# A column mean over 8192 rows: the last group of rows in five pieces instead of four, in three banks instead of two

## The chip, the cores and the metric

The kernel runs on one core of a Trainium2 chip. The metric is the device time of one execution in microseconds (us). Before the change the median of 3 runs is 628.02 us (628.0 to 628.23).

## The reference

```python
def setup_inputs():
    return {"x": np.random.randn(8192, 8192).astype(np.float32)}

def reference(x):
    return np.mean(x, axis=0)
```

The input is 256 MB of float32 (MB and KB count 1024 here, where rates and totals of the profile count 1000), and every byte of it has to be read once. The output is one row of 8192 values.

## The kernel before

The 8192 rows are 64 groups of 128 rows, one row of a group on each of the 128 partitions. A group is 8192 columns wide, 4 MB, and a column range of 512 (F) is called a block, so that a group has 16 blocks. Groups 0 to 59 are loaded in pairs, 8 MB in one DMA, and groups 60 to 63 singly (`strips`, L62 to L68, says which rows of the input stand in which group; for the sum it does not matter).

**Buffers.** `bufs` has six slots of one group. Four (0 to 3) take turns as landing places, two slots for a pair. The other two are `both` (slot 4) and `acc` (slot 5). Pair 0 is loaded straight into `both` and `acc`. An extra tile `early` takes blocks 0 to 5 of group 60, which are loaded at the start: two blocks ahead of pair 0 and four behind the first pairs (`load_early`).

**Loads.** All loads are issued by SyncE in program order on one DMA queue (`load`, L51). Those into slots that are reused wait for the VectorE add that read the slots last. Every second load from the ninth on waits also for two loads eight and seven places ahead, so that semaphores can be used again.

**Adds.** VectorE does the sums over groups (`add`, L78). Pairs 2, 4 and 6 are added to the two slots `both` and `acc` at once, each by one wide add of up to 16384 columns; the third leaves out blocks 0 and 1, which TensorE sums. Then `both` is added to `acc`. From group 8 on each pair takes two adds: `both` = slot u + slot u+1, then `acc` = `acc` + `both`. A load's add waits through a no-op on ScalarE or GpSimd (L83), which waits for the load and for the add before it. GpSimd adds `early` to `acc` in two parts, after groups 24 and 32.

**The sum over partitions.** TensorE multiplies a block by a 128 x 32 matrix of 1/8192 (`product`, L98). The result stands in one of four column groups of the array (q = 0 to 3, `tile_position`), 32 partitions of a PSUM bank; four blocks with different q share a bank of 512 columns. Each product shows as two weight loads and two matmuls in the profile. Banks 0, 1 and 2 hold blocks 0 to 11. Blocks 12 to 15 are cut differently: their 2048 columns are seen as four quarters (j) of 512 columns, each with four strips (q) of W = 128 columns, and a product takes the strips q of some quarters (`chunks`, L159). So a bank gets the first three quarters (bank 3, 384 columns) and another the last quarter (bank 4, 128 columns).

**The end.** VectorE adds only a part of groups 60 to 62 to `acc`; the other blocks, and all of group 63, go through TensorE directly. Group 63 is loaded in four pieces of 8, 4, 3 and 1 blocks. The list `sums` is the order in which TensorE works: blocks 0 to 5 of `acc` and of group 61, blocks 0 to 9 of group 62, blocks 6 and 7 of `acc`, blocks 0 to 7 of group 63, blocks 8 to 11 of `acc` and then of group 63, and the chunks of `acc` and of group 63. All engines keep program order. ScalarE then copies banks 0, 1 and 2 to `res` and bank 3 to `fin`, VectorE copies bank 4 to `fin`. ScalarE stores bank 0, SyncE stores banks 1 and 2 and, last, `fin`. Ahead of each store SyncE runs no-ops that wait for what the store needs (`landed`, L45), because one instruction can take few waits.

Of the kernel before, what the change touches and what calls it, by code (L numbers as in the profile page):

```python
# [9 lines left out]
def kernel(  # L10
# [9 lines left out]
    F = 512  # L20
    W = F // 4
# [19 lines left out]
    banks = [psp.tile([P, F], f32, name=f"bank{b}") for b in range(5)]  # L41
# [56 lines left out]
    def product(b, q, cols, start, stop):  # L98
        dst = banks[b][32 * q:32 * q + 32, :]
        if b > 2:  # L100
            dst = dst.rearrange("p (j w) -> p j w", w=W)[:, :cols.shape[1], :]
        return tc.keep_in_program_order(nc.tensor.matmul(  # L102
            out=dst,
            lhsT=ones[:],
            rhs=cols,
            start=start,
            stop=stop,
            tile_position=(0, 32 * q),
            skip_group_check=True,
        )).ins  # L110
# [6 lines left out]
    for g in range(2, G - 4, 2):  # L117
        u = (g + 2) % 4
        dma = load_rows(g, u, 2)
        if g < 8:  # L120
            cols = slice(0 if g < 6 else 2 * F, N)
            add(sums2[:, :, cols], sums2[:, :, cols], bufs[:, u:u + 2, cols], [dma] + first)
            first = []
            if g == 4:
                load_early(2, E)
            if g == 6:
                for q in range(2):
                    for j in range(2):
                        product(0, q, bufs[:, u + j, q * F:(q + 1) * F], j == 0, False)
                add(acc, acc, both, [])  # L130
            continue
        add(both, bufs[:, u, :], bufs[:, u + 1, :], [dma])
        add(acc, acc, both, ahead)
        ahead = []
        if g in (24, 32):
            cols = slice(0, 2 * F) if g == 24 else slice(2 * F, E * F)
            ins = tc.keep_in_program_order(nc.gpsimd.tensor_add(  # L137
                out=acc[:, cols], in0=acc[:, cols], in1=early[:, cols])).ins
            tc.add_to_no_dep_group("early", ins)
            ahead = [joined] = [ins]  # L140
# [3 lines left out]
    for row, g, lo in [(r60, G - 4, E * F), (r61, G - 3, 0)]:  # L144
        add(acc[:, cols], acc[:, cols], row[:, cols], [load(row[:, lo:], rows(g)[:, lo:])])

    dma = load(r62, rows(G - 2))
    cols = slice(10 * F, N)
    add(acc[:, cols], acc[:, cols], r62[:, cols], [dma])
    for lo, hi in [(0, 8), (8, 12), (12, 15), (15, 16)]:  # L150
        load(r63[:, lo * F:hi * F], rows(G - 1)[:, lo * F:hi * F])
# [3 lines left out]
    def blocks(row, lo, hi):  # L155
        for i in range(lo, hi):
            sums.append((i // 4, i % 4, row[:, i * F:(i + 1) * F]))

    def chunks(row, lo, hi):  # L159
        for q in range(4):  # L160
            cols = row[:, 12 * F:].rearrange("p (j q w) -> p q j w", j=4, q=4)[:, q, lo:hi, :]
            sums.append((3 + lo // 3, q, cols))
# [12 lines left out]
    for n, (b, q, cols) in enumerate(sums):  # L175
        summed = product(b, q, cols, all(k[:2] != (b, q) for k in [(0, 0), (0, 1)] + sums[:n]),
# [14 lines left out]
    copied = copy(fin[:, :3 * W], banks[3][:, :3 * W])  # L191
    ended = nc.vector.tensor_copy(out=fin[:, 3 * W:], in_=banks[4][:, :W]).ins  # L192
    landed(*joins.values())
    landed(loads[-6])
    landed(*loads[-5:-3])
# [6 lines left out]
    landed(*loads[-3:-1])  # L202
    landed(loads[-1], s0)
    landed(s1, summed)
# [33 lines left out]
```

## Time and profile before

| | |
|---|---|
| runs (median of 3) | 628.02 us |
| the profiled execution: its span from first to last instruction (the only time that the profile gives for it) | 626.3 us |
| load queue, share of 16 DMA engines | 99.2% |
| HBM read | 268.44 MB (of 1000), 429 GB/s over the span |
| VectorE busy | 527.7 us |
| TensorE matmuls busy | 18.3 us |
| ScalarE, GpSimd busy | 3.7 us, 7.4 us |
| add of 16384 columns, mean of two | 17.2 us |
| add of 14336 columns (the third wide add) | 15.1 us |
| add of 8192 columns, mean of 53 | 8.7 us |
| last pieces of group 63: 2048, 1024, 768, 256 KB, issue to landing | 21.3, 23.2, 24.7, 24.8 us |

How to read it: busy times of the engines overlap, so they don't add up to the span. The chain of waits follows the work that ended last back to the start; 70% of it are DMAs, 28% adds of VectorE, 1% matmuls. "Issue to landing" of a load includes the time that it stands in the queue behind earlier loads. PE is TensorE's matmul, PEld its weight load, DVE VectorE, ACT ScalarE, POOL GpSimd, SPq SyncE's queue.

### The profile page before, as it was taken

The page shows a single profiled execution, that of the slowest core. Times are in us where ns is not written, and L with a number is a line of the kernel's source. Part 1 is how long each engine was busy: PE and PEld are TensorE (multiplying, and loading weights), DVE is VectorE, ACT ScalarE, POOL GpSimd, SP SyncE. Part 2 cuts the span into 40 slices and gives each one's busy share as a digit, 9 for nine tenths or more (in the row PEclk, how much of TensorE's full clock was granted, in tenths as well). Part 3 has the DMA queues.
Part 4 walks back from the last instruction along what each step waited for, and adds up shares of the span by engine and source line. Part 5 has one row for each costly group of instructions (what it writes and reads, how often), then busy time and mean ns, then how long its engine had stood idle before and what let it go on. Part 6 is the DMA issues. An engine that isn't in the chain of part 4 may idle for free.

```text
span 626.3 us, 464 instructions
## 1 busy us (share of the span) xinstructions
PE 18.3 (3%) x120; PEld 4.6 (1%) x120; DVE 527.7 (84%) x60; ACT 3.7 (1%) x6; POOL 7.4 (1%) x8
## 2 busy tenths in 40 slices
PE   0000020000000000000000000000000000000035
PEld 0000000000000000000000000000000000000001
DVE  0028979999988998888988899988898888998895
ACT  0000000000000000000000000000000000000001
POOL 0000000000000000010000200000000000000000
PEclk9999999999999999999999999999999999999999
DMA  9999999999999999999999999999999999999997
GB/s 393 444 402 434 437 469 402 469 402 465 406 448 423 440 431 423 448 410 460 406 465 402 469 402 469 402 469 402 469 402 465 406 448 423 423 448 406 431 435 305
DMA packets 5658, 268.50 MB, mean 429 GB/s; under 512 B 636, under 2 KB 652, under 8 KB 1048
## 3 DMA queue, kind: packets, MB, share of 16 engines
q1 hardware_dynamic: 5648, 268.46, 99.2%
q8 instruction: 1, 0.02, 0.0%
q10 hardware_dynamic: 8, 0.01, 0.0%
q14 instruction: 1, 0.01, 0.0%
HBM read 268.44 MB, written 0.03 MB: 429 GB/s over the span
## 4 chain that ended last, share of the span: by engine, by line
DMA 70%; DVE 28%; PE 1%; SPq 0%; issue 0%; ACTq 0%; POOLq 0%
DMA bufs<-in_x_dram 70%; DVE bufs L80 28%; PE bank L102 1%; SPq L52 0%; ACTq L83 0%; DVE fin L192 0%; POOLq L83 0%
## 5 line engine op out<-in xcount | busy, mean ns | idle before, releaser
L80 DVE TENSOR_TENSOR bufs<-bufs 128x8192 f32<-128x8192 f32 (+4 forms) x59 | 527.4, 8939 | 92.2 <-POOLq L83 52.3
L102 PE MATMUL bank<-bufs,ones 128*32 128x512 f32 (+2 forms) x120 | 18.3, 634 | 605.0 <-DVE bufs L80 517.7
L137 POOL TENSOR_TENSOR bufs<-bufs,early 128x1024 f32<-128x1024 f32 (+1 forms) x2 | 6.8, 3416 | 350.0 <-DVE bufs L80 350.0
L102 PEld LDWEIGHTS bank<-bufs,ones 128*32 128x32 f32 x120 | 4.6, 120 | 618.5 <-issue 610.7
L182 ACT COPY bufs<-bank 128x512 f32<-128x512 f32 x3 | 1.8, 586 | 618.2 <-PE bank L102 618.2
L192 DVE COPY fin<-bank 128x128 f32<-128x128 f32 x1 | 0.3, 292 | 3.8 <-PE bank L102 3.8
L115 ACT ACT_TABLE_LOAD x1 | 1.3, 1283 | 0.7 <-PEq L222 0.7
L182 ACT COPY fin<-bank 128x384 f32<-128x384 f32 x1 | 0.5, 480 | 1.0 <-PE bank L102 1.0
L115 ACT COPY warm<-ones 128x32 f32<-128x32 f32 x1 | 0.2, 217 | 0.0
L40 POOL TENSOR_TENSOR ready<-ones 128x1 f32<-128x1 f32 x1 | 0.2, 192 | 0.1
L37 POOL MEMSET ones<- 128x32 f32 x1 | 0.1, 124 | 0.3 <-POOLq L222 0.3
L222 POOL MEMSET const-bfloat16-1.0<- 128x1 bf16 x1 | 0.1, 101 | 0.0
L222 POOL MEMSET const-uint8-127<- 128x1 uint8 x1 | 0.1, 101 | 0.0
L222 POOL MEMSET const-float32-0.0<- 128x1 f32 x1 | 0.1, 98 | 0.2 <-issue 0.2
L222 POOL MEMSET const-float32-1.0<- 128x1 f32 x1 | 0.1, 98 | 0.0
## 6 DMA issues: line engine op xcount, KB each, us to landing
bufs<-in_x_dram SPq DMA_DIRECT2D x2, 4096.0 KB, 16.7
bufs<-in_x_dram SPq DMA_DIRECT2D x1, 2560.0 KB
bufs<-in_x_dram SPq DMA_DIRECT2D x1, 2048.0 KB, 21.3
early<-in_x_dram SPq DMA_DIRECT2D x1, 1024.0 KB, 62.0
bufs<-in_x_dram SPq DMA_DIRECT2D x1, 1024.0 KB, 23.2
bufs<-in_x_dram SPq DMA_DIRECT2D x1, 768.0 KB, 24.7
early<-in_x_dram SPq DMA_DIRECT2D x1, 512.0 KB
bufs<-in_x_dram SPq DMA_DIRECT2D x30, 29.9
```

The lines of the kernel that those rows point to most:

```text
L37: nc.gpsimd.memset(ones[:], 1.0 / M)
L40: nc.gpsimd.tensor_add(out=ready[:], in0=ones[:, 0:1], in1=ones[:, 1:2]))
L80: ins = tc.keep_in_program_order(nc.vector.tensor_add(out=dst, in0=a, in1=b)).ins
L102: return tc.keep_in_program_order(nc.tensor.matmul(out=dst, lhsT=ones[:], rhs=cols, start=start, stop=stop, tile_position=(0, 32 * q), ski ...
L115: tc.keep_in_program_order(nc.scalar.copy(out=warm[:], in_=ones[:]))
L137: ins = tc.keep_in_program_order(nc.gpsimd.tensor_add(out=acc[:, cols], in0=acc[:, cols], in1=early[:, cols])).ins
L182: return tc.keep_in_program_order(nc.scalar.copy(out=dst, in_=src)).ins
L192: ended = nc.vector.tensor_copy(out=fin[:, 3 * W:], in_=banks[4][:, :W]).ins
L222: nc = _bacc.Bacc("TRN2", target_bir_lowering=False, num_devices=1)
```

## The change

- `W` is 64 instead of 128 columns: blocks 12 to 15 are now eight slices (j) of 256 columns with four strips of 64.
- Group 63 is loaded in five pieces of 8, 4, 2.5, 1 and 0.5 blocks. The last three have banks of their own: bank 3 with 320 columns, bank 4 with 128, bank 5 with 64. ScalarE copies banks 3 and 4 to `fin`, VectorE bank 5.
- TensorE sums blocks 0 to 11 of group 62 (before: 0 to 9), and all blocks 6 to 11 of `acc` ahead of group 63 (before: 6 and 7). The chunks of `acc` come ahead of blocks 8 to 11 of group 63. VectorE's add of group 62 has blocks 12 to 15 (before: 10 to 15).
- The third wide add takes all 16384 columns, and TensorE's four products of group 6 are gone.
- The second part of `early`, four blocks, is loaded in two halves, one issued behind pair 4 and one behind pair 6.
- The last store writes runs of 64 columns (256 bytes) instead of 128. SyncE has one no-op more behind it.

```diff
-    W = F // 4
+    W = F // 8
...
-    banks = [psp.tile([P, F], f32, name=f"bank{b}") for b in range(5)]
+    banks = [psp.tile([P, F], f32, name=f"bank{b}") for b in range(6)]
...
         if g < 8:
-            cols = slice(0 if g < 6 else 2 * F, N)
-            add(sums2[:, :, cols], sums2[:, :, cols], bufs[:, u:u + 2, cols], [dma] + first)
+            add(sums2[:], sums2[:], bufs[:, u:u + 2, :], [dma] + first)
             first = []
-            if g == 4:
-                load_early(2, E)
+            if g > 2:
+                load_early(g - 2, g)
             if g == 6:
-                for q in range(2):
-                    for j in range(2):
-                        product(0, q, bufs[:, u + j, q * F:(q + 1) * F], j == 0, False)
                 add(acc, acc, both, [])
...
     dma = load(r62, rows(G - 2))
-    cols = slice(10 * F, N)
+    cols = slice(12 * F, N)
     add(acc[:, cols], acc[:, cols], r62[:, cols], [dma])
-    for lo, hi in [(0, 8), (8, 12), (12, 15), (15, 16)]:
-        load(r63[:, lo * F:hi * F], rows(G - 1)[:, lo * F:hi * F])
+    for lo, hi in [(0, 16), (16, 24), (24, 29), (29, 31), (31, 32)]:
+        cols = slice(lo * F // 2, hi * F // 2)
+        load(r63[:, cols], rows(G - 1)[:, cols])
...
+    parts = [0, 5, 7, 8]
+
     def chunks(row, lo, hi):
+        b = max(k for k in range(3) if parts[k] <= lo)
         for q in range(4):
-            cols = row[:, 12 * F:].rearrange("p (j q w) -> p q j w", j=4, q=4)[:, q, lo:hi, :]
-            sums.append((3 + lo // 3, q, cols))
+            cols = row[:, 12 * F:].rearrange("p (j q w) -> p q j w", j=8, q=4)[:, q, lo:hi, :]
+            sums.append((3 + b, q, cols, lo - parts[b]))

     blocks(acc, 0, 6)
     blocks(r61, 0, 6)
-    blocks(r62, 0, 10)
-    blocks(acc, 6, 8)
+    blocks(r62, 0, 12)
+    blocks(acc, 6, 12)
     blocks(r63, 0, 8)
-    blocks(acc, 8, 12)
+    for lo, hi in zip(parts, parts[1:]):
+        chunks(acc, lo, hi)
     blocks(r63, 8, 12)
-    chunks(acc, 0, 3)
-    chunks(acc, 3, 4)
-    chunks(r63, 0, 3)
-    chunks(r63, 3, 4)
+    for lo, hi in [(0, 5), (5, 7), (7, 8)]:
+        chunks(r63, lo, hi)
...
-    copied = copy(fin[:, :3 * W], banks[3][:, :3 * W])
-    ended = nc.vector.tensor_copy(out=fin[:, 3 * W:], in_=banks[4][:, :W]).ins
+    copy(fin[:, :5 * W], banks[3][:, :5 * W])
+    copied = copy(fin[:, 5 * W:7 * W], banks[4][:, :2 * W])
+    ended = nc.vector.tensor_copy(out=fin[:, 7 * W:], in_=banks[5][:, :W]).ins
...
     landed(copied)
-    ins = store(nc.sync, out[12 * F:].rearrange("(j q w) -> q j w", j=4, q=4),
+    ins = store(nc.sync, out[12 * F:].rearrange("(j q w) -> q j w", j=8, q=4),
           fin[0:P:32, :].rearrange("q (j w) -> q j w", w=W))
```

More of the change, by code (lines that the diff above doesn't have):

```diff
@@ L96, in load_early, with product @@
         load(early[:, lo * F:hi * F], rows(G - 4)[:, lo * F:hi * F])
-    def product(b, q, cols, start, stop):
+    def product(b, q, cols, at, start, stop):
         dst = banks[b][32 * q:32 * q + 32, :]
         if b > 2:
-            dst = dst.rearrange("p (j w) -> p j w", w=W)[:, :cols.shape[1], :]
+            dst = dst.rearrange("p (j w) -> p j w", w=W)[:, at:at + cols.shape[1], :]
         return tc.keep_in_program_order(nc.tensor.matmul(
@@ L143 @@
     cols = slice(E * F, N)
-    for row, g, lo in [(r60, G - 4, E * F), (r61, G - 3, 0)]:
-        add(acc[:, cols], acc[:, cols], row[:, cols], [load(row[:, lo:], rows(g)[:, lo:])])
+    add(acc[:, cols], acc[:, cols], r60[:, cols], [load(r60[:, E * F:], rows(G - 4)[:, E * F:])])
+    dma = load(r61, rows(G - 3))
+    add(acc[:, cols], acc[:, cols], r61[:, cols], [dma])
     dma = load(r62, rows(G - 2))
-    cols = slice(10 * F, N)
+    cols = slice(12 * F, N)
     add(acc[:, cols], acc[:, cols], r62[:, cols], [dma])
-    for lo, hi in [(0, 8), (8, 12), (12, 15), (15, 16)]:
-        load(r63[:, lo * F:hi * F], rows(G - 1)[:, lo * F:hi * F])
+    for lo, hi in [(0, 16), (16, 24), (24, 29), (29, 31), (31, 32)]:
+        cols = slice(lo * F // 2, hi * F // 2)
+        load(r63[:, cols], rows(G - 1)[:, cols])
     sums = []
@@ L156, in blocks @@
         for i in range(lo, hi):
-            sums.append((i // 4, i % 4, row[:, i * F:(i + 1) * F]))
+            sums.append((i // 4, i % 4, row[:, i * F:(i + 1) * F], 0))
+    parts = [0, 5, 7, 8]
     def chunks(row, lo, hi):
+        b = max(k for k in range(3) if parts[k] <= lo)
         for q in range(4):
-            cols = row[:, 12 * F:].rearrange("p (j q w) -> p q j w", j=4, q=4)[:, q, lo:hi, :]
-            sums.append((3 + lo // 3, q, cols))
+            cols = row[:, 12 * F:].rearrange("p (j q w) -> p q j w", j=8, q=4)[:, q, lo:hi, :]
+            sums.append((3 + b, q, cols, lo - parts[b]))
     blocks(acc, 0, 6)
     blocks(r61, 0, 6)
-    blocks(r62, 0, 10)
-    blocks(acc, 6, 8)
+    blocks(r62, 0, 12)
+    blocks(acc, 6, 12)
     blocks(r63, 0, 8)
-    blocks(acc, 8, 12)
+    for lo, hi in zip(parts, parts[1:]):
+        chunks(acc, lo, hi)
     blocks(r63, 8, 12)
-    chunks(acc, 0, 3)
-    chunks(acc, 3, 4)
-    chunks(r63, 0, 3)
-    chunks(r63, 3, 4)
-    for n, (b, q, cols) in enumerate(sums):
-        summed = product(b, q, cols, all(k[:2] != (b, q) for k in [(0, 0), (0, 1)] + sums[:n]),
+    for lo, hi in [(0, 5), (5, 7), (7, 8)]:
+        chunks(r63, lo, hi)
+    for n, (b, q, cols, at) in enumerate(sums):
+        summed = product(b, q, cols, at, all(k[:2] != (b, q) for k in sums[:n]),
                          all(k[:2] != (b, q) for k in sums[n + 1:]))
@@ L190 @@
         copy(res[:, b, :], banks[b][:])
-    copied = copy(fin[:, :3 * W], banks[3][:, :3 * W])
-    ended = nc.vector.tensor_copy(out=fin[:, 3 * W:], in_=banks[4][:, :W]).ins
+    copy(fin[:, :5 * W], banks[3][:, :5 * W])
+    copied = copy(fin[:, 5 * W:7 * W], banks[4][:, :2 * W])
+    ended = nc.vector.tensor_copy(out=fin[:, 7 * W:], in_=banks[5][:, :W]).ins
     landed(*joins.values())
-    landed(loads[-6])
-    landed(*loads[-5:-3])
+    landed(loads[-7])
+    landed(*loads[-6:-4])
     landed(joined)
@@ L198 @@
     landed(copied)
-    ins = store(nc.sync, out[12 * F:].rearrange("(j q w) -> q j w", j=4, q=4),
+    ins = store(nc.sync, out[12 * F:].rearrange("(j q w) -> q j w", j=8, q=4),
           fin[0:P:32, :].rearrange("q (j w) -> q j w", w=W))
     tc.declare_no_dep(ins, copied, reason="the no-op waited")
-    landed(*loads[-3:-1])
-    landed(loads[-1], s0)
-    landed(s1, summed)
+    landed(*loads[-4:-2])
+    landed(*loads[-2:])
+    landed(s0, s1)
+    landed(summed)
     landed(ended)
```

## The prediction

> **What bounds the kernel now.** I read the page first, then the chain of waits in order of time at both ends, then the timeline of the last microseconds and the groups kept apart by shape.
>
> ```profile
> span 626.3 us, 464 instructions
> ...
> PE 18.3 (3%) x120; PEld 4.6 (1%) x120; DVE 527.7 (84%) x60; ACT 3.7 (1%) x6; POOL 7.4 (1%) x8
> ...
> DMA  9999999999999999999999999999999999999997
> ...
> q1 hardware_dynamic: 5648, 268.46, 99.2%
> ```
>
> The load queue is busy for 99.2% of the span on all 16 engines, so the idle remainder is 0.8% of 626.3 = 5.0 us. The trace's packet records put it at the two ends: the first packet starts at 1.77, the last load lands at 622.88, 3.4 us before the end, and in between no engine stands still. Only the amount of data, the cost of cutting it into loads, an interruption of the stream, and the tail behind the last landing can move the time. VectorE at 84% is no limit unless it releases a buffer too late.
>
> The chain of waits at the start:
>
> ```profile
> 42.86 17.23 DVE bufs L80
> 60.09 0.02 issue
> 60.11 23.90 DMA bufs<-in_x_dram
> 84.01 0.04 ACTq L83
> 84.05 0.02 issue
> 84.07 15.10 DVE bufs L80
> 99.17 0.02 issue
> 99.20 8.70 DVE bufs L80
> ```
>
> The first wide add frees two buffers, at 60.11 SyncE issues group 6 into them, and it lands at 84.01. The third wide add ends at 99.17 and releases the load of group 10 (issued 99.25, landed 122.98).
>
> The timeline of the end, and the groups with shapes kept apart:
>
> ```profile
> 617.92 0.16 PEld L102 LDWEIGHTS bank<-bufs,ones 128*32 128x32 f32 x8 [1.59 <-DMA bufs<-in_x_dram]
> ...
> 620.40 0.25 PEld L102 LDWEIGHTS bank<-bufs,ones 128*32 128x32 f32 x8 [0.61 <-DMA bufs<-in_x_dram]
> ...
> 622.93 0.17 PEld L102 LDWEIGHTS bank<-bufs,ones 128*32 128x32 f32 x8 [0.47 <-DMA bufs<-in_x_dram]
> 623.22 0.48 ACT L182 COPY fin<-bank 128x384 f32<-128x384 f32 x1 [1.00 <-PE bank L102]
> 623.44 0.29 DVE L192 COPY fin<-bank 128x128 f32<-128x128 f32 x1 [3.84 <-PE bank L102]
> 623.77 0.54 SPq L185 DMA_DIRECT2D out_dram<-fin  x1
> ```
> ```profile
> L102 PE MATMUL bank<-bufs,ones 128*32 128x384 f32 x16 | 1.7, 492 | 0.0
> L102 PE MATMUL bank<-bufs,ones 128*32 128x128 f32 x16 | 0.8, 273 | 0.0
> ```
>
> The four loads of the last group land at 617.88, 620.36, 622.25 and 622.88; TensorE starts 0.04 to 0.05 us after the first. The last path is: landing 622.88, matmuls 622.97 to 623.37, VectorE's copy to 623.73, the store issued 623.77 to 624.31 and complete at 625.50, closing barriers to 626.26.
>
> **The change part by part.** The sum is made against this execution's span, 626.26; the page gives no other time for it. The timed runs have a median of 628.02, so 1.76 lies around the span, and I keep that.
>
> *Two more loads.* The second early load of 1 MB becomes two of 0.5 MB, and the last group goes in five pieces (2048, 1024, 640, 256, 128 KB) instead of four; the bytes are the same. Price of a cut: 2048 KB took 4.90 us after its predecessor, 1024 KB 2.48. With b us per MB and a per load, 2b + a = 4.90 and b + a = 2.48, so b = 2.42 and a = 0.06. This gives 1.88 for 768 KB (measured 1.89) and 0.67 for 256 KB (0.63). Two more loads: +0.12, ends 0 and +0.2. The pieces then land at 617.94, 620.42, 621.99, 622.66 and 623.00. Their issues, three of some 0.4 us near 597, have 20 us of cover; the early one stands on SyncE right behind group 6's load, ahead of a load released only at 79.48.
>
> A rule of the Trainium skill speaks against small loads: "DMA: Bandwidth & Descriptors", section Bandwidth, advises batches of at least 1 MiB, and the section on the anatomy of a DMA gives each (on the GpSimd path) some 2.0 us fixed. By it two more loads would cost an estimated 4 us; by the row they cost 0.12. The trace disagrees where loads are queued: 256 KB landed 0.63 us after the load ahead.
>
> *Third wide add whole, four early products gone.* The add grows from 15.10 us to the 17.22 of the first two. Half of the early megabyte no longer stands ahead of group 6, so that lands about 1.2 us earlier, at 82.8. The add ends at 82.86 + 17.22 = 100.1, 0.9 later, and so does the release of group 10's load. Its cover: group 8 is in the queue until about 103.4 in both kernels, so issue to end of queue shrinks from 4.1 to 3.3 us. At group 6 it shrinks from 64.61 - 60.11 = 4.5 to 3.3. What a late load needs: the first loads, issued at 0.74 on an idle queue, had 16.5 MB landed at 42.80; at the steady 19.35 us per 8 MB that is 39.9 of transfer and 2.1 of issue, start and landing. 2.1 is under 3.3, so I cost this at nothing. Behind it VectorE is 0.9 later for its backlog; it waits 4.6 us for group 6 and gains 1.9 per pair, and group 12's load, at 117.6 instead of 116.7, has over 5 us. If the cover were gone, see the rival. TensorE loses 3.63 us at 84 that nobody waited for, and group 10's load loses its wait for them.
>
> *Sums ahead of the last group.* Of group 62 TensorE takes 12 blocks instead of 10, and acc 6 to 11 instead of 6 and 7. The four column groups run side by side (four blocks take two steps of 0.43 us), so 12 blocks fit the same six steps, 613.03 to 615.8. Acc 6 to 11 start at 616.19 and need four steps, to 617.91; the next landing is at 617.94. Cost 0; at worst some 0.1 late, which the pause below takes up. VectorE's last add has 2048 columns instead of 3072 and ends at 618.6 instead of 619.60, and acc's twelve chunk products (about 0.95 us by 0.85 ns a column) now precede the last four whole blocks. TensorE: eight blocks to 619.7, chunks to 620.65, four blocks to 621.5, idle until 622.0. So it is not late for the last pieces; without this order it would be, as it is by 0.04 now.
>
> *The last piece, half as wide.* TensorE starts 0.05 after the landing instead of 0.09: -0.04. 128 columns took 273 ns, 384 took 492: 0.855 ns a column, so 64 take 218 (-0.055), and the second step starts 0.055 instead of 0.11 after the first. Together -0.11; if weight loads (0.17 for eight) set the step, -0.05. VectorE's copy: 64 columns less at the 1.04 ns a column of its adds, 292 to 225 ns: -0.07.
>
> *One copy more on ScalarE, and a wait on it.* ScalarE copies 320 columns, then 128, in front of the store. The 640 KB piece lands at 621.99, its products end near 622.75, the copy (480 less 64 x 0.83 = 427 ns) runs 622.82 to 623.25; the second (about 270 ns) 623.29 to 623.56. VectorE ends at 623.00 + 0.05 + 0.29 + 0.07 + 0.225 = 623.64. ScalarE is done 0.08 earlier: 0 on the path, at worst +0.15. The store of banks 1 and 2 ahead on SyncE ends near 623.0. The extra no-op behind the last store (0.06) lies beside its 1.2 us of flight.
>
> *The last store* moves 32 runs of 256 B instead of 16 of 512 B. Nothing here shows such a store. Its runs took 25 to 32 ns each, four on each of four engines, so eight shorter ones add some 0.04; issuing took 0.54 here and 0.70 for the other store on SyncE. I take +0.05, nearest to the packet row; ends -0.05 and +0.5.
>
> The same page's Specifications table gives 512 B as the least for line rate, with read-modify-write below. By it the 0.11 us of runs would at a guess double, an estimated +0.1 instead of +0.05; no run here shows a 256 B run.
>
> *Sum:* +0.12 - 0.04 - 0.11 - 0.07 + 0.05 = -0.05, so a span of 626.2 and a time of 628.0. 0.2% is 1.26 us, about what a measurement of this kernel can tell from no change.
>
> **The rivals.**
>
> 1. *The queue runs dry at groups 6 and 10: slower.* For: both loads' cover shrinks by 0.8 to 1.2, and at 102.8, where group 10 begins now, a few packets took 2.55 to 2.88 us instead of 2.42. Against: 2.1 of 3.3 is needed, and packets follow each other there without a gap. It decides once a late load needs more than 3.3 us. Today's cover of 4.1 suffices, so at most 0.8 is lost at each place, 1.6 together: 629.6. To pass 0.2% the need must exceed 3.9.
>
> 2. *The last store is slow in short runs.* Its flight behind the issue is 1.19 us. Doubled, with an issue of 0.70: +1.3, 629.3. For: nothing shows such runs. Against: packets are 0.11 of the 1.19.
>
> 3. *Every load has a fixed price that queueing does not hide.* By the first loads' 2.1 us each, two more cost 4.2: 632.1. The landings above speak against it. This is the page's batching rule as a mechanism.
>
> 4. *The tail gains more,* each piece being copied from its own bank while the next lands. Matmuls and copy behind the last landing are 0.85 us in all; half of it gone is 627.6. The stream allows no more, so over 0.2% faster needs a tail shorter by 1.3.
>
> **How the numbers follow.** Forecast as summed 0.73 (627.7 to 628.4), rival 4 0.10, rival 1 0.10 (half of it above 629.28), rival 2 0.05 (mostly below that line), rival 3 0.02. Faster by over 0.2%: 0.03, for a tail read wrongly; slower: 0.05 + 0.02 + 0.02, and 0.01 for a mishap unseen, 0.10; within: 0.87. Range 627.6 to 628.7: down to rival 4, up by the store's +0.5 and half of a dry spell.
>
> **What would show it.** The load queue without a pause at 63 and 103; group 6 landed near 82.8, the third wide add ending near 100.1; last landing at 623.0; two last matmul steps under 0.1 apart; VectorE's copy about 225 ns, ending behind ScalarE's; the last store issued near 623.7. Wrong would be: a pause of the queue in the first 105 us, a store over 2 us from issue to completion, or ScalarE's second copy ending last.

## The result: a last load that comes late in most executions

The changed kernel takes 629.66 us (median of 22 runs, 627.74 to 630.42) against 628.24 us (median of 22, 627.93 to 628.81) for the kernel before, taken beside it. Over all runs the ratio is 1.0016, 95% interval 1.0011 to 1.0022. (This ratio, like those below, is taken over all the runs and is not that of the two medians, which is 1.0023.) That is inside the 0.2% that I had called the limit of a measurement, but the median lies 1.4 us above the kernel before and above the range of the forecast. The median hides the shape. Six runs of the changed kernel lie between 627.74 and 628.50, where the forecast was; the other sixteen between 629.08 and 630.42. The kernel before has no such upper group: none of its 158 runs, taken beside the changed kernel and all the experiments below, is over 629.0. The profiled execution of the changed kernel (629.93 us, span 628.1) belongs to the upper group, so its trace shows what the forecast missed.

The page of the profile after, the lines that answer to those shown of before:

```profile
span 628.1 us, 491 instructions
...
PE 15.8 (3%) x132; PEld 4.4 (1%) x132; DVE 528.7 (84%) x60; ACT 3.9 (1%) x7; POOL 7.4 (1%) x8
...
DMA  9999999999999999999999999999999999999996
...
q1 hardware_dynamic: 5952, 268.46, 99.0%
q8 instruction: 1, 0.02, 0.0%
```

The load queue is as busy as before; the last slice alone moves less (257 GB/s instead of 305). The line of queue 8 stands in the page of before too:

```profile
q8 instruction: 1, 0.02, 0.0%
```

It is one packet of 16 KB, it carries instructions of an engine and not data, and I had passed it over.

The chain of waits at the start, after:

```profile
42.96 17.24 DVE bufs L80
60.20 0.02 issue
60.21 22.86 DMA bufs<-in_x_dram
83.07 0.03 ACTq L83
83.11 0.02 issue
83.13 17.24 DVE bufs L80
100.37 0.02 issue
```

Group 6 lands at 83.07 and the third wide add ends at 100.37, both within 0.3 us of the forecast. The first piece of the last group lands at 617.89 (before: 617.88), so nothing was lost up to there.

The chain at the end, and the timeline of the last microseconds, both after:

```profile
598.51 25.86 DMA bufs<-in_x_dram
624.37 0.04 issue
624.41 0.36 PE bank L102 x8
624.78 0.02 issue
624.80 0.23 DVE fin L193
```
```profile
622.01 0.16 PEld L102 LDWEIGHTS bank<-bufs,ones 128*32 128x32 f32 x8 [1.33 <-DMA bufs<-in_x_dram]
622.01 1.11 PE L102 MATMUL bank<-bufs,ones 128*32 128x320 f32 x16 [0.42 <-DMA bufs<-in_x_dram]
...
622.82 0.63 ACT L182 COPY fin<-bank 128x320 f32<-128x320 f32 x2 [0.58 <-PE bank L102]
624.41 0.16 PEld L102 LDWEIGHTS bank<-bufs,ones 128*32 128x32 f32 x8 [1.57 <-DMA bufs<-in_x_dram]
624.41 0.32 PE L102 MATMUL bank<-bufs,ones 128*32 128x64 f32 x8 [1.30 <-DMA bufs<-in_x_dram]
624.80 0.23 DVE L193 COPY fin<-bank 128x64 f32<-128x64 f32 x1 [6.27 <-PE bank L102]
625.17 0.55 SPq L185 DMA_DIRECT2D out_dram<-fin  x1
```

The pieces land at 617.89, 620.38, 621.97, 622.65 and 624.37; the forecast had 617.94, 620.42, 621.99, 622.66 and 623.00. Four are right to 0.05 us, and the fifth, the smallest, is 1.4 late. Ahead of its products the matmuls have stood still for 1.30 us (the weight loads for 1.57), waiting for that load.

The span grew by 1.82 us, and it splits like this (before, after):

| step | before | after | difference |
|---|---|---|---|
| last landing | 622.88 | 624.37 | +1.49 |
| from there to the end of VectorE's copy | 0.85 | 0.66 | -0.19 |
| to the start of the last store's issue | 0.04 | 0.14 | +0.10 |
| the issue | 0.54 | 0.55 | +0.01 |
| from its end to completion | 1.19 | 1.60 | +0.41 |
| closing | 0.76 | 0.76 | 0 |

The trace's packet records show the cause of the first row. A load has landed when its sixteen semaphore increments, one for each DMA engine, have arrived. Fifteen of the last load's have arrived by 622.94; the last of these was written at 622.49, some 0.45 earlier. Queue 8's packet of 16,384 bytes starts at 622.18 and takes 1.11 us, to 623.29; the two 1 KB packets of the load that are still missing start at 623.27 and 623.38 and take 125 and 138 ns (elsewhere 46), and the sixteenth increment is written at 623.51. It arrives at 624.37, 0.86 and not 0.45 later. So of the lateness about 1.0 us are packets that came late, and 0.4 an increment that took longer to arrive. The records name no engine, but the two packets and the increment come just when the long packet ends. In the trace of before the same packet starts at 622.12 and takes 1.08 us, and no load packet comes behind it, so nobody waits. The slow arrival of the increment is in other late landings too (1.10 in e2 and 0.88 in f1, but 0.44 in g1 and 0.50 in h4; these kernels follow below), and I have no cause for it.

So the question for the experiments is whose instructions these are, and what brings the fetch ahead of the load's last packets.

### The profile page after: what moved, and what is told of

The parts are those of the page before. It is cut to its first block, busy times and chain, and to the rows that moved or that the text cites. A ratio compares the mean times of both kernels' runs of the same rounds, so it can differ in the third digit from the quotient of the medians.

```text
span 628.1 us, 491 instructions
## 1 busy us (share of the span) xinstructions
PE 15.8 (3%) x132; PEld 4.4 (1%) x132; DVE 528.7 (84%) x60; ACT 3.9 (1%) x7; POOL 7.4 (1%) x8
## 4 chain that ended last, share of the span: by engine, by line
DMA 70%; DVE 28%; SPq 0%; issue 0%; ACTq 0%; PE 0%; POOLq 0%
DMA bufs<-in_x_dram 70%; DVE bufs L80 28%; SPq L52 0%; ACTq L83 0%; PE bank L102 0%; DVE fin L193 0%; POOLq L83 0%
## 5 line engine op out<-in xcount | busy, mean ns | idle before, releaser
L80 DVE TENSOR_TENSOR bufs<-bufs 128x8192 f32<-128x8192 f32 (+3 forms) x59 | 528.4, 8956 | 90.1 <-POOLq L83 52.6
L102 PE MATMUL bank<-bufs,ones 128*32 128x512 f32 (+3 forms) x132 | 15.8, 565 | 608.9 <-DVE bufs L80 605.4
```

Source lines behind the costliest of these rows:

```text
L80: ins = tc.keep_in_program_order(nc.vector.tensor_add(out=dst, in0=a, in1=b)).ins
L102: return tc.keep_in_program_order(nc.tensor.matmul(out=dst, lhsT=ones[:], rhs=cols, start=start, stop=stop, tile_position=(0, 32 * q), ski ...
```

## The experiments

Where several of the theories below are named in an expectation, these are they. Theory 1: the fetch belongs to ScalarE's program. Theory 2: packets of 1 KB are late by themselves. Theory 3: the fetch follows something else. Theory 4: the new head of the kernel (whole third wide add, early loads moved) is what costs. Theory 5: only short runs let the fetch in. Theory 6: the fetch belongs to TensorE's program. Theory 7: it is asked for when TensorE reaches a certain place in its program, and the new order of products reaches it earlier, while loads still run. "Before" stands for the kernel before, "after" for the changed one. All times are in us.

### One instruction less or more on ScalarE

`e1_act_one_less`, an edit of after, moves one waiting no-op from ScalarE to GpSimd; `e2_act_one_more` moves one the other way, and `e4_before_act_more` is the same edit of before.

```diff
# e1
-            waiter = nc.scalar if len(adds) % 8 > 1 else nc.gpsimd
+            waiter = nc.scalar if len(adds) % 8 > 1 and len(adds) != 44 else nc.gpsimd
# e2, and e4 in the kernel before
-            waiter = nc.scalar if len(adds) % 8 > 1 else nc.gpsimd
+            waiter = nc.scalar if len(adds) % 8 > 1 or len(adds) == 48 else nc.gpsimd
```

> The changed kernel with one no-op of an add in mid-run (add 44) moved from ScalarE to GpSimd, so that ScalarE's program is one instruction shorter; nothing else. Theory 1: the 16 KB instruction fetch (queue 8, 622.18 in the changed kernel, 1.1 us on one DMA engine) is ScalarE's own and starts at a fixed place in its program, and two packets of the last piece stood behind it. One instruction less makes it start one instruction later, with the copy of bank 3 (622.8 + 0.5 = about 623.3), behind the last load. So the last piece lands near 623.0 in the profile, and the times have one cluster at 627.7 to 628.5, ratio to before about 0.9995. Theory 2, a last piece of 1 KB rows is late by itself: landing near 624.4, most times 629 to 630.4 as in the changed kernel. Theory 3, the fetch follows something else (ScalarE's store, the time): fetch at 622.2 again, times as in the changed kernel, median near 629.7.

> The changed kernel with one no-op (add 48) moved from GpSimd to ScalarE, so that ScalarE's program is one instruction longer. Theory 1: the fetch starts one instruction earlier, with the copy of bank 1 (620.8 + 0.5 = about 621.3), amid the load stream, so it always delays one DMA engine by about its 1.1 us: every run slow, 629 to 630.4, last piece near 624 in the profile, no cluster at 628. Theories 2 and 3: fetch at 622.2, both clusters, as in the changed kernel.

> The kernel before, with one no-op (add 48) moved from GpSimd to ScalarE and nothing else. Theory 1: the fetch moves from 622.12 to about 621.3, into the load stream, and one DMA engine ends 1.1 us late: all runs about 1 us above the kernel before, 629.0 to 629.6, last landing near 624 in the profile, with no piece of 1 KB rows at all. Theories 2 and 3: no change, 628.2.

Measured: e1 629.27 (628.22 to 631.19, 12 runs), ratio 1.0015, 95% interval 1.0007 to 1.0024. e2 628.61 (628.07 to 630.18, 11 runs), 1.0006 (0.9997 to 1.0014). e4 628.43 (627.98 to 628.85, 11 runs), 1.0001 (0.9992 to 1.0009). The fetch starts at 622.03, 621.98 and 622.12. Had it hung on ScalarE's count, one instruction less or more would have moved it to that engine's next instruction or the one before, about 623.3 or 621.3; it stays. Theory 1 falls. The profile of e1 fell into the lower group: the same fetch, but no load packet behind it, and the last piece lands at 623.21, 5.04 behind the first (forecast 5.06). So 1 KB packets are not late by themselves, and theory 2 falls as well. In e2's profile only a semaphore write of 4 bytes stood behind the fetch, and the last landing was late all the same (624.18).

### Four pieces instead of five

`e3_four_pieces`, an edit of after, keeps its head and TensorE's order and joins the last two pieces.

```diff
-    for lo, hi in [(0, 16), (16, 24), (24, 29), (29, 31), (31, 32)]:
+    for lo, hi in [(0, 16), (16, 24), (24, 30), (30, 32)]:
...
-    parts = [0, 5, 7, 8]
+    parts = [0, 6, 8]
```

> The changed kernel with the last group in four pieces as before (8, 4, 3 and 1 blocks) and so in two banks (384 and 128 columns); the wide add, the early halves, TensorE's order and the store in runs of 256 bytes stay as changed. Theory 1: the stream ends 0.08 us earlier against ScalarE's work, which follows the landing at 617.9, so its last packets are mostly ahead of the fetch at 622.15 again, as in the kernel before: median 627.9 to 628.6, few or no runs above 629. Theory 2 expects the same, since the 1 KB rows are gone. If the half megabytes or the whole wide add were the cause, the times stay at 629 to 630.4. The store in short runs should take about 1.6 us from the end of its issue to its completion, as in the changed kernel (1.19 before), if that was the run length and not chance.

Measured: 630.43 (628.53 to 631.38, 7 runs), ratio 1.0026 (1.0016 to 1.0037), the wrong way for theory 2: with the last cut undone it is no better. Its profile is from a run near the bottom (628.88; last landing 623.29, fetch at 621.97), so it shows no late packet; it does show single packets of 3.21 us at 63.0 and 2.93 us at 102.6, the places of groups 6 and 10, where the others take 2.4. That made the head a suspect, the mechanism of the first rival of the prediction.

### The head by itself

Four kernels. `f1_head_before` is after with the old head (third wide add without blocks 0 and 1, four early products, one early megabyte). The others are before with one part of the new head: `f2_before_halves` splits the early megabyte, `f3_before_whole_add` takes the whole third add but leaves the early megabyte in one piece ahead of group 6, `f4_before_early_late` moves that megabyte behind pair 6.

```diff
# f1, in the changed kernel
-            add(sums2[:], sums2[:], bufs[:, u:u + 2, :], [dma] + first)
+            cols = slice(0 if g < 6 else 2 * F, N)
+            add(sums2[:, :, cols], sums2[:, :, cols], bufs[:, u:u + 2, cols], [dma] + first)
...
-            if g > 2:
-                load_early(g - 2, g)
+            if g == 4:
+                load_early(2, E)
             if g == 6:
+                for q in range(2):
+                    for j in range(2):
+                        product(0, q, bufs[:, u + j, q * F:(q + 1) * F], 0, j == 0, False)
# f2, in the kernel before
-            if g == 4:
-                load_early(2, E)
+            if g > 2:
+                load_early(g - 2, g)
# f3, in the kernel before
-            cols = slice(0 if g < 6 else 2 * F, N)
-            add(sums2[:, :, cols], sums2[:, :, cols], bufs[:, u:u + 2, cols], [dma] + first)
+            add(sums2[:], sums2[:], bufs[:, u:u + 2, :], [dma] + first)
...
-                for q in range(2):
-                    for j in range(2):
-                        product(0, q, bufs[:, u + j, q * F:(q + 1) * F], j == 0, False)
# f4, in the kernel before
-            if g == 4:
+            if g == 6:
                 load_early(2, E)
```

> The changed kernel with its first 130 us as before: the second early part in one load of 1 MB behind pair 4, the third wide add without blocks 0 and 1, which TensorE sums. The end (five pieces, three banks, order of TensorE, short runs) stays as changed. Theory 4 (cover): in the changed kernel the loads of groups 6 and 10 are issued only 2.7 and 2.5 us before the queue reaches them (3.9 and 3.5 before), and then the first packet of a DMA engine is at times slow (up to +0.8 us seen in profiles); an engine never makes this up, so the last landing, or the packets that stand behind the instruction fetch at 622.1, come later. With the head as before the spread goes: one cluster, 627.7 to 628.6, ratio to before 0.9995. Theory 1 alone (the fetch meets the last 1 KB piece, whatever the head): both clusters stay, median 629 to 629.7.

> The kernel before with the second early part in two halves, behind pairs 4 and 6, and nothing else. Theory 4: group 6 is issued 2.7 us before its turn instead of 3.9, group 10 as before; some runs slow, median 628.6 to 629.5, some slow first packets near 63. Theory 1 alone: as before but 0.07 later, 628.3 to 628.5.

> The kernel before with the third wide add whole and without TensorE's four early products, and nothing else. The early megabyte stands ahead of group 6, which lands at 84.0, so the add ends at 101.3 and group 10 is issued about 1.5 us before the queue reaches it at 102.8 (3.5 before, 2.5 in the changed kernel). Theory 4: the worst of all, slow first packets at 103 on several engines, median 629.5 to 631. Theory 1 alone, or the 1.0 us that the very first load took from issue to first packet as the whole need: no change, 628.2 to 628.5.

> The kernel before with the whole second early part (1 MB) loaded behind pair 6 instead of pair 4. Group 6 then follows group 4 in the queue, at 61.6, and is issued at 60.1, 1.5 us before its turn; group 10 gains cover (its add ends 2.4 us earlier, its turn is the same). Theory 4: slow first packets at 61.6, none at 103, median 629.5 to 631. Theory 1 alone: no change, 628.2 to 628.5.

Measured:

| | median (range, runs) | ratio (95%) |
|---|---|---|
| f1 | 629.84 (628.01 to 630.07, 11) | 1.0010 (1.0001 to 1.0019) |
| f2 | 628.47 (628.11 to 629.35, 11) | 1.0002 (0.9993 to 1.0010) |
| f3 | 630.64 (629.78 to 631.12, 5) | 1.0032 (1.0020 to 1.0045) |
| f4 | 628.90 (628.40 to 629.29, 11) | 1.0007 (0.9999 to 1.0016) |

With the old head the upper group is still there (f1: six of eleven runs at 629.84 to 630.07), so the head does not make it. But the head's mechanism is real. In f3, where group 6 keeps its old landing and the add is longer, the chain of waits has the third add end at 101.53:

```profile
84.24 0.03 ACTq L83
84.27 0.02 issue
84.30 17.23 DVE bufs L80
101.53 0.02 issue
```

Group 10 is issued then, at 101.55, and the load ahead of it lands at 103.59: by the prediction's measure, from issue to the end of the queue ahead, a cover of 2.0. (The expectations count to the first packet of the load itself, which gives less.) The first packets of its load take 2.6 to 3.4 us on nearly all the DMA engines instead of 2.4. The last group lands at 625.71 instead of 622.88, and all five runs are over 629.7. In f4 group 6's load has a cover of 2.0 as well (issued 60.22, landing ahead 62.25), and its first packets take 2.6 to 3.2 on some fourteen engines, for a loss of half a microsecond. At the cover of the changed kernel, 3.5 at group 6 and 3.3 at group 10, only single packets are slow (after: four of 2.5 to 2.7 at group 6, none at group 10). So theory 4 explains little of the result.

### The rest of the change, part by part

`g1_head_before_four` is e3 with the old head of f1: of the change, the products' order, the narrower strips and the short store are left. `g2_fewer_products` is after without TensorE's 18 products of groups 61 and 62; it leaves their sums out of the output. `g3_before_last_halved` is before with its last piece cut in two, one bank for both; `i2_halved_again` is the same kernel measured a second time. `g4_before_new_head` is before with the whole new head.

```diff
# g2, in the changed kernel
     blocks(acc, 0, 6)
-    blocks(r61, 0, 6)
-    blocks(r62, 0, 12)
     blocks(acc, 6, 12)
# g3 and i2, in the kernel before
-    for lo, hi in [(0, 8), (8, 12), (12, 15), (15, 16)]:
-        load(r63[:, lo * F:hi * F], rows(G - 1)[:, lo * F:hi * F])
+    for lo, hi in [(0, 16), (16, 24), (24, 30), (30, 31), (31, 32)]:
+        cols = slice(lo * F // 2, hi * F // 2)
+        load(r63[:, cols], rows(G - 1)[:, cols])
...
```

> The changed kernel with the head as before and the last group in four pieces (8, 4, 3, 1 blocks, two banks): what is left of the change is TensorE's order (12 blocks of group 62, blocks 6 to 11 of acc and its chunks ahead), strips of 64 columns and the store in runs of 256 bytes. Theory 5: the 16 KB fetch waits on its DMA engine until the load queue leaves a gap there, and only among runs of 1 KB does a gap come before the piece is through; so with 2 KB runs and the old head no run is slow: one cluster, 628.1 to 628.7, the fetch 0.01 us behind a semaphore write in the profile. If TensorE's order or the store is to blame: a second cluster above 629.5.

> The changed kernel without TensorE's products of group 61 (blocks 0 to 5) and group 62 (blocks 0 to 11), whose sums are thus missing from the output; TensorE's program is 72 instructions shorter, the loads, adds, copies and stores are the same. Theory 6: the fetch is for TensorE's program (its 66 products are 264 instructions and more, and 16 KB hold 256 of 64 bytes), so with 192 none is fetched on queue 8 in the last microseconds, and the slow cluster is gone; TensorE starts slower behind a pause, which may cost some 0.5 us, so one cluster between 627.7 and 629. Against it: fetch at 622.0 again, two clusters 1.8 us apart.

> The kernel before with its last piece (1 block, 2 KB runs) loaded in two of half a block (1 KB runs), same banks, same order. Theory 5: now a gap among the 1 KB runs lets the fetch in ahead of the last packets in some runs: two clusters, about 628.3 and 630.1, a third of the runs or more in the upper. A theory in which the smaller banks or the order make it: one cluster, 628.3 to 628.6 (one more cut, +0.07).

> The kernel before with the changed head alone: early part in halves behind pairs 4 and 6, third wide add whole, no early products. Group 6 is issued 2.7 us and group 10 2.5 us before its turn. Theory 4 together with the four-piece run of the changed kernel (628.5 to 631.4): a broad spread, 628.4 to 631, median near 629.5 to 630.4, slow first packets (2.9 to 3.2 us) near 63 and 103. If the four-piece run was slow for its end: one cluster at 628.4.

Measured:

| | median (range, runs) | ratio (95%) |
|---|---|---|
| g1 | 628.51 (628.38 to 630.44, 11) | 1.0012 (1.0003 to 1.0021) |
| g2 | 630.01 (629.73 to 630.93, 7) | 1.0029 (1.0018 to 1.0039) |
| g3 | 628.05 (628.01 to 628.50, 11) | 0.9998 (0.9989 to 1.0007) |
| g4 | 628.46 (628.19 to 629.30, 11) | 1.0004 (0.9996 to 1.0013) |
| i2 | 628.23 (627.88 to 628.55, 11) | 0.9998 (0.9989 to 1.0007) |

g1 has both groups, seven runs at 628.38 to 628.52 and four at 630.08 to 630.44. Its profile is of the upper group, with four packets of 2 KB behind the fetch:

```profile
624.41 0.16 PEld L102 LDWEIGHTS bank<-bufs,ones 128*32 128x32 f32 x8 [2.00 <-DMA bufs<-in_x_dram]
```

Its last landing is at 624.37, as in the changed kernel, with runs as long as before's. So theory 5 falls. The new order of the products, the narrower strips and the short store are what f1, e3 and the changed kernel have in common with it, and g3, g4 and f2 have not.

g2 says whose instructions they are. Only TensorE's program is shorter, and the fetch is gone from the span. The view of its DMA queues:

```profile
## 3 DMA queue, kind: packets, MB, share of 16 engines
q1 hardware_dynamic: 5952, 268.46, 99.1%
q10 hardware_dynamic: 8, 0.01, 0.0%
q14 instruction: 1, 0.01, 0.0%
```

The last piece lands at 622.85, the earliest of the kernels with this cutting. The time is no better for it, against the expectation of 627.7 to 629. From the last landing to the last store's issue it is 1.67 instead of 0.80. And the packet records have the fetch at 628.73, behind the span of 627.03; what lies around the span is 2.70 in this run and 2.93 and 2.95 in two others. In the other four it is 1.90 to 2.06, as in the other kernels (1.74 to 2.30), and the span is 627.7 to 628.4; they have no trace. Theory 6 holds, and with it what was general in theory 3: the fetch belongs to TensorE's program.

### TensorE's order by itself, and undone

`h1_before_new_order` is before with the new order of products (and VectorE's smaller add of group 62) alone. `h2_before_short_strips` is before with strips of 64 columns and the short store alone. `h3_chunks_back` is after with one step of the order undone: the chunks of `acc` come behind blocks 8 to 11 of group 63 again. `h4_before_more_products` is before with six more products, done at 84 us when TensorE has nothing else, into bank 2, which is written anew later.

```diff
# h1, in the kernel before
-    cols = slice(10 * F, N)
+    cols = slice(12 * F, N)
...
-    blocks(r62, 0, 10)
-    blocks(acc, 6, 8)
+    blocks(r62, 0, 12)
+    blocks(acc, 6, 12)
     blocks(r63, 0, 8)
-    blocks(acc, 8, 12)
-    blocks(r63, 8, 12)
     chunks(acc, 0, 3)
     chunks(acc, 3, 4)
+    blocks(r63, 8, 12)
# h3, in the changed kernel
     blocks(r63, 0, 8)
+    blocks(r63, 8, 12)
     for lo, hi in zip(parts, parts[1:]):
         chunks(acc, lo, hi)
-    blocks(r63, 8, 12)
# h4, in the kernel before
             if g == 6:
+                for k in range(6):
+                    product(2, k % 4, bufs[:, u, k * F:(k + 1) * F], True, True)
```

> The kernel before with the changed order of TensorE alone: 12 blocks of group 62, blocks 6 to 11 of acc and acc's chunks ahead of blocks 8 to 11 of group 63 (VectorE's last add 2048 columns). Head, four pieces of 2 KB runs and more, strips of 128, store in runs of 512 bytes as before. Theory 7: the fetch of TensorE's program is asked for when TensorE passes a place some 170 to 200 instructions into it; in the new order it passes it about 1.5 us earlier (620.5 instead of 622.0), while the load queue is still at work on that DMA engine, and then it can push in ahead of the last packets. So two clusters, 628.3 and 630.1, a third to two thirds of the runs in the upper. If the strips of 64 or the short runs of the store make it: one cluster, 628.2 to 628.6.

> The kernel before with strips of 64 columns and so a store in runs of 256 bytes, nothing else. Theory 7: one cluster, 628.3 to 628.8; the store from the end of its issue to completion 1.2 us, or 1.6 if short runs are slow. If strips or store make the slow runs: two clusters, 628.4 and 630.1.

> The changed kernel with one move undone: acc's chunks again behind blocks 8 to 11 of group 63. Theory 7: TensorE passes the place 48 instructions later in its program's time, near 621.9 as before, so the upper cluster goes or shrinks to a run or two: 627.8 to 628.6. TensorE is not late by it: blocks to 620.5 and 621.3, chunks to 622.3 (0.3 behind the landing of the 640 KB piece), so at most 0.1 on the end. If the five pieces, the head or the store make it: half of the runs or more at 629.5 to 630.4 again.

> The kernel before with six products more for TensorE at 84 us, when it is idle (group 6 into bank 2, overwritten later), 24 instructions; the last 20 us are untouched but for the place in the program. Theory 7: TensorE passes any fixed place 24 instructions earlier, about 1.3 us in that stretch (620.7 instead of 622.0), so the upper cluster appears with no change to loads, adds, order or stores: 628.3 and 630.1, a third of the runs or more in the upper. Against it: one cluster, 628.2 to 628.6.

Measured:

| | median (range, runs) | ratio (95%) |
|---|---|---|
| h1 | 628.97 (628.32 to 630.42, 11) | 1.0015 (1.0006 to 1.0024) |
| h2 | 628.51 (628.20 to 628.94, 11) | 1.0001 (0.9992 to 1.0010) |
| h3 | 628.62 (628.20 to 629.75, 11) | 1.0005 (0.9996 to 1.0014) |
| h4 | 630.24 (629.84 to 630.56, 6) | 1.0029 (1.0018 to 1.0041) |

The order alone, put into the kernel before, makes the upper group (h1: four of eleven runs at 629.53 to 630.42). One step of it undone nearly takes it from the changed kernel (h3: one run, 629.75). The profile of h1 is of a run in the lower group (628.32; fetch at 621.86, no load packet behind it), so its upper group is known by its times alone. The short strips and the short store do nothing (h2).

h4 leaves order, cutting and store as before and adds 24 instructions to TensorE's program at a time when TensorE is idle. The fetch comes at 621.24, 0.9 earlier (0.65 earlier counted from the first piece's landing), the loads of the 768 and 256 KB pieces are both held up (one 6 KB packet behind the fetch takes 654 ns instead of 237), and every run is over 629.8. The timeline of h4:

```profile
623.58 0.16 PEld L102 LDWEIGHTS bank<-bufs,ones 128*32 128x32 f32 x8 [1.65 <-DMA bufs<-in_x_dram]
...
624.21 0.17 PEld L102 LDWEIGHTS bank<-bufs,ones 128*32 128x32 f32 x8 [0.48 <-DMA bufs<-in_x_dram]
```

Its pieces land at 623.53 and 624.17, where before has 622.25 and 622.88. Work without any cost of its own, 540 us ahead of the end, costs 1.9 us there.

### All of the end but the order

`i1_pieces_old_order` is before with the five pieces, three banks, strips of 64 and short store of the change, and with the old head and TensorE's old order (the chunks for the third bank added at the end).

```diff
-    for lo, hi in [(0, 8), (8, 12), (12, 15), (15, 16)]:
-        load(r63[:, lo * F:hi * F], rows(G - 1)[:, lo * F:hi * F])
+    for lo, hi in [(0, 16), (16, 24), (24, 29), (29, 31), (31, 32)]:
+        cols = slice(lo * F // 2, hi * F // 2)
+        load(r63[:, cols], rows(G - 1)[:, cols])
...
     blocks(r62, 0, 10)
     blocks(acc, 6, 8)
     blocks(r63, 0, 8)
     blocks(acc, 8, 12)
     blocks(r63, 8, 12)
-    chunks(acc, 0, 3)
-    chunks(acc, 3, 4)
-    chunks(r63, 0, 3)
-    chunks(r63, 3, 4)
+    for lo, hi in zip(parts, parts[1:]):
+        chunks(acc, lo, hi)
+    for lo, hi in [(0, 5), (5, 7), (7, 8)]:
+        chunks(r63, lo, hi)
...
```

> The kernel before with the five pieces, three banks, strips of 64 and the short store of the change, but the old head and the old order of TensorE (10 blocks of group 62, acc's blocks 8 to 11 and chunks late). Theory 7: TensorE is as far in its program as before at 622, so no slow cluster: 627.8 to 628.5, ratio to before 0.9990 to 1.0000. If five pieces do matter for the fetch: a quarter of the runs or more at 629.5 to 630.4.

> The kernel before with only its last piece in two halves, a second time: the earlier runs gave a median of 628.05 against 628.34. If that holds, 627.9 to 628.3, ratio 0.9995; if it was the draw of runs, 628.3 to 628.5. Theory 7 expects no slow cluster in either case.

Measured: i1 628.06 (627.74 to 628.76, 11 runs) against 628.37 (627.82 to 629.0, 21 runs), ratio 0.9997 (0.9988 to 1.0005); no upper group. The last products follow the load at once, and all copies end together:

```profile
623.20 0.48 PEld L102 LDWEIGHTS bank<-bufs,ones 128*32 128x32 f32 x16 [0.28 <-DMA bufs<-in_x_dram]
623.57 0.59 ACT L187 COPY fin<-bank 128x320 f32<-128x320 f32 x2 [0.82 <-PE bank L102]
623.91 0.23 DVE L198 COPY fin<-bank 128x64 f32<-128x64 f32 x1 [3.78 <-PE bank L102]
624.28 0.54 SPq L190 DMA_DIRECT2D out_dram<-fin  x1
```

The last load lands at 623.48, 5.06 behind the first piece as forecast. TensorE's matmuls run without a break from 618.46 to the end, as they did in the kernel before, and are not late: the order that the change brings was not needed for the five pieces. i1 and i2 are no measurable gain over the kernel before; no kernel here is.

### All runs together

When does TensorE start its 161st recorded matmul or weight load, counted from the landing of the first piece of the last group? I chose the measure after the runs, and the line of 629.4 too. Every count from 153 to 184 sorts the kernels into the same groups; at lower counts h3 falls in with the changed kernel. f3 (late from its head) and g2 (no fetch in the span) are left out.

| 161st instruction, us after the first piece's landing | kernels | runs over 629.4 |
|---|---|---|
| 0.94 | f1, g1, h1, h4 | 20 of 39 |
| 1.80 | after, e1, e2, e3 | 28 of 52 |
| 2.52 to 2.56 | e4, f2, f4, g3, h2, h3, i1, i2 | 1 of 88 |
| 3.09 | g4 | 0 of 11 |
| 2.52 | before, all its runs | 0 of 158 |

With TensorE at that place by 1.80 us, half of the runs are over 629.4; from 2.52 on, one in 257. That is what theory 7 says. It does not order the kernels any finer: h1 and h4 are alike by it, and differ as four of eleven to six of six. Nor does TensorE's granted clock explain the groups: of the 136 runs of the kernel before in these experiments 70 had 0.58 to 0.59 of the full clock, and none was over 629.0, while the upper groups of f1 and h1 have both kinds.

A page of the Trainium skill bears on it. "Runtime: NRT & Kernel Launch", section Instruction fetch mechanics, says that an engine's instruction memory is refilled in blocks of 16 KiB, 256 instructions, which its sequencer fetches over a DMA queue of its own while it executes the current block, and calls the cost mostly hidden. The traces agree on the size (one packet of 16,384 bytes on queue 8). "Mostly hidden" holds for the kernel before, and not where the block comes among the last packets of the load that everything waits for: +1.49 us.

Another page of the Trainium skill, "DMA: Bandwidth & Descriptors", section Queues, rings and completion order, says that a DMA engine takes turns between queues that have work, packet by packet, where its packet is a group of typically 9 to 17 descriptors. That would let a fetch pass ahead of load packets that are already waiting, as the two at 623.27 and 623.38 did; no run here shows which queue's turn it was.

**What stays open.** The moment of the fetch by itself does not tell the groups apart: it starts at 622.12 in before and 622.18 in after, and in e1 and e3 at 622.0 without harm, so whether packets of the last load are then left on that one DMA engine differs from run to run. Counted from the first piece's landing it starts 3.59 to 4.26 later in the kernels of the table's first row, 3.68 to 4.28 in those of the second and 3.76 to 4.43 in the others, so the ranges overlap. No trace records when the block is asked for. So the step from an earlier place in the program to a fetch ahead of the last packets is argued from the table and from h4, and not shown. The exact place in TensorE's program was not found, nor why e3 has the highest median of the kernels with the new order, nor why four of eleven runs of h1 are in the upper group and all of h4's. The last store's flight is another: in the five profiles where the fetch delayed the landing (after, e2, f1, g1, h4) it takes 1.60 to 1.91, in four with runs of 256 B and in h4 with 512 B, and in all others 1.18 to 1.21. In after its packets are on time (the last semaphore write 0.85 behind the issue, before 0.84), and the 0.41 come later: the last of its four increments arrives 0.73 behind its write, the other three 0.37. It is the same kind of slow arrival as at after's last load.

## Why the prediction was wrong, and where it was right

- **"Sums ahead of the last group ... Cost 0"**: this step failed. As work the order was hidden, as I wrote: in after, the matmuls stood waiting 0.42 us for the 640 KB piece and 1.30 for the last. (It was not needed either: i1 without it has the same 0.80 from landing to store as e1.) But the step counted only what TensorE executes. Its program is data too, 16 KB at a time on the DMA engines that carry the input, and with the new order this packet comes, in many runs, ahead of the last packets of the load: +1.49 at the last landing in after. Put into the kernel before, the step that I priced at 0 cost 0.9 us (0.4 to 1.5) over all runs (h1, ratio 1.0015). That the order makes the upper group is shown by h1 (this step alone), h3 (a part of it undone) and i1 (everything else of the end without it); that the fetch is TensorE's, by g2 and h4. That it comes about by an earlier request is theory 7, which fits and is not shown. The line of queue 8 stood in the profile of before, 622.12 to 623.20 in the records, and I passed it over.
- **"Only the amount of data, the cost of cutting it into loads, an interruption of the stream, and the tail"**: the list was right, and the result is an interruption of the stream. I had looked for one only in the first 105 us, and my list of what would prove me wrong did not have it. Of that list one thing did come, a store of over 2 us from issue to completion (2.15 in after); but its packets were on time, and h4 with runs of 512 B has it too.
- **Two more loads, +0.12**: right in the sum. From the first piece to the last landing it is 5.00 in before, 5.04 in e1, 5.06 in i1, forecast 5.06. The third rival, a fixed price per load (632.1), is refuted by i1 for one load more and by the lower group of the changed kernel for both.
- **Third wide add whole, cost 0**: nearly right. Group 6 landed at 83.07 and the add ended at 100.37 (forecast 82.8 and 100.1), and the cover at group 10 is the 3.3 that I had worked out. But 2.1 us is no sharp need. With 2.0, a tenth less, f4 lost half a microsecond and f3's last landing came 2.8 later, and at 3.3 to 3.5 single first packets still are slow; g4, this whole part alone, has four of eleven runs at 628.98 to 629.30 and a ratio of 1.0004. The first rival's mechanism exists, at 0.1 to 0.3 us (medians and ratio of g4) and not 1.6.
- **Last piece half as wide, -0.11 and -0.04 and -0.07**: right to 0.03. From landing to the end of VectorE's copy it is 0.66 instead of 0.85; VectorE's copy takes 225 ns.
- **One copy more on ScalarE, 0**: right in after, where the second copy ends at 623.45, long before the late piece; in i1 the last ends 0.04 behind VectorE's copy and not 0.08 ahead of it.
- **Last store, +0.05**: the runs of 256 B cost nothing (flight 1.20 in e1 and h2, 1.19 before), so the second rival falls. What was missing is 0.10 ahead of the issue: from the end of VectorE's copy to the store it is 0.14 in every kernel with three banks but g2 (0.39) and 0.04 in every one with two, with two semaphore instructions of SyncE between (625.05 to 625.13 in after). So the whole tail from landing to issue gained 0.09 and not 0.22.
- **Sum, 628.0**: what the undisturbed runs show (627.74 to 628.50), and i1's 628.06. The fourth rival, a tail that gains more, is not seen: from the last landing to the end of the span it is 3.38 in before, 3.30 in e1 and 3.31 in i1.

The chance of 0.87 for "within 0.2%" fits the ratio over all runs, 1.0016, though its interval reaches 1.0022; but the median of 629.66 is above the range, whose upper end, 628.7, took in only half a dry spell and a slow store.

## What to carry to other kernels

An engine's own instructions are fetched over the same DMA engines as the data, so a reordering or a few more instructions, even idle ones half a millisecond earlier, can put a 16 KB packet in front of the last load's last packets (after and h4): look at the instruction queues of the profile and at when they run, wherever the end hangs on a landing. Each load is spread over the 16 DMA engines and lands with the last of them, so a delay on one is a delay of all. A load that must not break the stream has to be issued well before the load ahead of it lands: with 2.0 us nearly all its first packets were slow here, with 3.3 to 3.5 single ones. And look at the single runs before the median: two groups of runs are a cause that sometimes strikes, and a mean over them is the time of no execution.

## What the runs showed of the hardware

- A packet of instructions of 16 KB holds its DMA engine for 1.02 to 1.26 us, and packets right behind it take about 2.7 to 3 times as long as others: 124 to 138 ns instead of 46 for 1 KB (after, f1), 228 to 231 instead of 84 for 2 KB (g1), 654 instead of 237 for 6 KB (h4).
- In g2's profiled run the block of TensorE's instructions is not fetched within the span but behind it, at 628.73, and the time around the span is 2.70 us, where the changed kernel's profiled run has 1.85.
- A semaphore increment behind a fetch can take longer to arrive: 0.86 to 1.10 us from its write in after, e2 and f1, where the others of the same load take some 0.45; in g1 and h4 it takes 0.44 and 0.50.
- A load issued 2.0 us before the load ahead of it lands has slow first packets on nearly every DMA engine (2.6 to 3.4 us instead of 2.4 in f3 and f4), though the queue ahead of it is not empty, and what an engine loses there it does not make up in the 520 us that follow (f3: last landing 625.71 instead of 622.88).
